# A hybrid encoder step on one core: TensorE's queue in the order in which the code emits it

## The chip, the core and the metric

The kernel runs on one core of one Trainium2 chip. The metric is the device time of one execution in microseconds (us); the time of a kernel is the median of its runs. The core has five engines with a queue each: TensorE (PE, with its weight loads as PEld), VectorE (DVE), ScalarE (ACT), GpSimd (POOL) and SyncE (SP), which here issues the transfers.

## What is computed

One layer of a streaming encoder, over a prompt of 2048 tokens and a sample of 32 tokens, all in float32. One projection yields the streams of two mixers: HGRN2, a gated recurrence of 4 heads evaluated in chunks of 64 tokens, and FoX, a causal attention of 8 heads with a forget gate. Then come an output projection, a second norm and a feed-forward block of width 4096.

```python
def mixer_inputs(x, norm1, w_in, ...):
    z = rms_norm(x, norm1) @ w_in
    qa, fa, ia, ga, qb, kb, vb, fb = jnp.split(z, SPLITS, axis=-1)
    ...
def mixer_output_and_ffn(x, o_a, ga, o_b, hgrn_out_norm, w_out, norm2, w_up, w_down):
    oa = rms_norm(o_a, hgrn_out_norm.reshape(A_HEADS, A_DV))
    oa = oa.reshape(B, T, A_WIDTH) * jax.nn.silu(ga)
    x = x + jnp.concatenate([oa, o_b], axis=-1) @ w_out
    h = rms_norm(x, norm2)
    return x + jnp.square(jax.nn.relu(h @ w_up)) @ w_down
```

The outputs are both sequences, the new keys, values and log forget values, and the recurrent states.

## The kernel before

**Tiles.** The prompt is cut into four quarters of 512 tokens; the third (`SQ`) carries the 32 sample tokens too and is worked in two pieces of 272. A dense product is made of three matmuls for each tile of 128 rows of weights (`mm3`): weights and activations are split into a rounded high part and the rest (`wh`, `wl`, `ahi`, `alo`), and high times high, high times low and low times high are added in one PSUM bank. `load_w` (L158) loads a weight strip, ACT rounds it to `wh` (L163), POOL subtracts to get `wl` (L165).

**PSUM.** Four pools share the eight banks: `ps_x` with three buffers (scores `st`, maxima `mx`, the recurrence's `xa`, `xu`, `xo`), `ps_o` with one (the attention's output `ot`), `ps_mm` with two for dense products, `ps_tr` with two for transposes (`ta`, `tk`, `tv`, `th`, `mt`, ...). Before the output projection, at L1327 and L1328, `ps_mm` and `ps_tr` are opened anew with three buffers and one.

**The flow.** All work is written as Python generators, and `Flow` (L41) decides in which order their instructions are emitted. It keeps a clock `flow.t` that only `mm` (L94) and `tp` (L102) advance, by an assumed time for each matmul or transpose. `dense` runs the main stream (strips of products) and, after each of its steps, everything whose due time has come: a generator that yields `lat` is taken up again `lat` us of that clock later. `until` runs only what is due until a condition holds. So the tails of a strip (transposes, norms, stores), the attention's steps and the norms are strewn between the matmuls of the strips.

**What sets the order on the engines.** What is emitted first has priority. But each engine's queue is written by the scheduler of the framework: it goes through the instructions with assumed durations, and when an engine is free it gives it the earliest emitted instruction that it takes to be ready, a later one where the earlier ones are not. The queue is fixed when the program is built; on the chip an engine goes through it in order, waiting on semaphores.

**Lines that the prediction follows.** `to_acts` (L190) transposes 128 tokens of the normed rows in two groups of four `ta`, with ACT's copy (L197) and DVE's subtraction (L198) behind each. `gate_tail` (L339) transposes the forget gate into `tl`, which ACT copies (L375). `att_max` (L828) takes row maxima, puts their negatives into `mpad` on DVE (L843, L844) and transposes them into `mt`. `out_tail` (L1083) and `y_tail` (L1165) bring a strip of the third quarter back to rows: four transposes, an add on DVE (L1087, L1175), then one more transpose for the sample tokens, in a new tile of the same pool:

```python
tr = ps_tr.tile([P, 4, P], F32, tag="tr", ...)
for i in range(4):
    tp(tr[:, i, :], ob[:, i * P:(i + 1) * P], ident)
dve.tensor_tensor(x2[:, :, cs], x2[:, :, cs], tr, op=ALU.add)
...
tr = ps_tr.tile([P, 4, P], F32, tag="tr", ...)
tp(tr[0:TS, 0, :], ob[:, 512:544], ident)
```

`ffn` (L1099) runs `up` (two strips of 128 of the 4096 columns) and `down` of the pair before in turn; after the last pair `down` follows at once.

Of the kernel before, what the change touches and what calls it, by code (L numbers as in the profile page):

```python
# [75 lines left out]
def hymba_step(  # L76
# [76 lines left out]
    def rstd(out, ss, n, cnt):  # L153

        pool.tensor_scalar(out, ss, 1.0 / cnt, EPS, op0=ALU.mult, op1=ALU.add)
        pool.tensor_tensor(out, out, phalf[0:out.shape[0], 0:n], op=ALU.pow)
# [22 lines left out]
    def nid():  # L179
        uid[0] += 1  # L180
        return uid[0]

    def new_acts(q):
        n = QN[q]
        u = nid()
        hi = acts.tile([P, KT, n], F32R, tag="ahi", name=f"ahi{u}")
        lo = acts.tile([P, KT, n], F32R, tag="alo", name=f"alo{u}")
        return hi, lo

    def to_acts(row, w, hi, lo, t0):  # L190

        for g in range(row.shape[1] // 512):
            tr = ps_tr.tile([P, 4, P], F32, tag="tr", name=f"ta{nid()}")
            for j in range(4):
                kt = 4 * g + j
                tp(tr[:, j, 0:w], row[0:w, kt * P:(kt + 1) * P], ident[0:w, 0:w])
            act.copy(hi[:, 4 * g:4 * g + 4, t0:t0 + w], tr[:, :, 0:w])  # L197
            dve.tensor_tensor(lo[:, 4 * g:4 * g + 4, t0:t0 + w], tr[:, :, 0:w],  # L198
                              hi.bitcast(F32)[:, 4 * g:4 * g + 4, t0:t0 + w], op=ALU.subtract)
            yield TLAT  # L200
# [6 lines left out]
    def load_gain(src):  # L207
        gb = const.tile([P, D], F32, tag="gbc", name=f"gbc{nid()}")
        sp.dma_start(gb, src.partition_broadcast(P))
        return gb  # L210
# [4 lines left out]
    def build(q, done, gb, getrow, src=None, first=False):  # L215

        while row_use:
            yield 0.5
        row_use.append(1)
        hi, lo = new_acts(q)  # L220

        if first:

            src = acts.tile([P, 4, D], F32, tag="ahi", name="stage")
            for i, (t0, w) in enumerate(QT[q]):
                sp.dma_start(src[:, i, :], getrow(q, t0, w))
                if i == 0:
                    gb = load_gain(norm1[0])
                    gains.append(gb)

        def prep(t0, w):
            if src is not None and t0 < 512:
                x = src[:, t0 // P, :]
                row = x if first else rows.tile([P, D], F32, tag="row", name=f"row{nid()}")
            else:
                row = rows.tile([P, D], F32, tag="row", name=f"row{nid()}")
                x = row
                sp.dma_start(row[0:w, :], getrow(q, t0, w))
            ss = small.tile([P, 2], F32, tag="ss", name=f"ss{nid()}")
            for g in range(2):  # L240
                junk = rows.tile([P, 512], BF16, tag="junk", name=f"junk{nid()}", bufs=1)
                act.activation(junk[0:w, :], x[0:w, 512 * g:512 * g + 512], AF.Square,
                               accum_out=ss[0:w, g:g + 1])
            r = small.tile([P, 1], F32, tag="rs", name=f"rs{nid()}")
            pool.tensor_tensor(r[0:w, :], ss[0:w, 0:1], ss[0:w, 1:2], op=ALU.add)
            rstd(r[0:w, :], r[0:w, :], 1, D)
            dve.scalar_tensor_tensor(out=row[0:w, :], in0=x[0:w, :], scalar=r[0:w, :],  # L247
                                     in1=gb[0:w, :], op0=ALU.mult, op1=ALU.mult)
            return row, w, t0

        lat = BLAT
        ts = QT[q]
        cur = prep(*ts[0])
        for i in range(len(ts)):
            nxt = prep(*ts[i + 1]) if i + 1 < len(ts) else None
            yield lat if i == 0 else lat - 3.0
            row, w, t0 = cur
            yield from to_acts(row, w, hi, lo, t0)
            cur = nxt
        done[q] = (hi, lo)  # L260
        row_use.clear()
# [938 lines left out]
    def heads(qs, hs, late=False):  # L1200
# [9 lines left out]
        for g in gates:  # L1210
            yield from g

    flow.spawn(build(0, A, None, xrow, None, True))
    flow.until(lambda: 0 in A)

# [142 lines left out]
    flow.until(lambda: 3 in H)  # L1358
    flow.dense(ffn(3, H, X, ffp))
    flow.until(lambda: not flow.q)  # L1360


# [31 lines left out]
```

## Time and profile before

| | |
|---|---|
| median of 3 runs | 2978.21 us (2977.03 to 2981.14) |
| the profiled execution | 2982.22 us, span 2980.5 us |
| TensorE matmuls busy | 2875.0 us, 96% |
| weight loads busy | 2435.9 us, 82% |
| VectorE, ScalarE, GpSimd busy | 62%, 46%, 37% |
| DMA queue of SP | 379.15 MB, 43.6% of 16 engines |

All rows are from one profiled execution. Its span runs from the first to the last recorded instruction, and times of places are counted from the span's start. In a timeline a row gives start, duration, engine, line, operation, out<-in, shapes and count, and in brackets the idle time of the engine before it with what ended it. Matmuls are pipelined: a row of TensorE lasts longer than the distance to the next one, so distances are taken from start to start. The granted clock is the share of TensorE's full 2.4 GHz that it was given; 0.50 is 1.2 GHz.

### The profile page before, as it was taken

The page shows a single profiled execution, that of the slowest core. Times are in us where ns is not written, and L with a number is a line of the kernel's source. Part 1 is how long each engine was busy: PE and PEld are TensorE (multiplying, and loading weights), DVE is VectorE, ACT ScalarE, POOL GpSimd, SP SyncE. Part 2 cuts the span into 40 slices and gives each one's busy share as a digit, 9 for nine tenths or more (in the row PEclk, how much of TensorE's full clock was granted, in tenths as well). Part 3 has the DMA queues.
Part 4 walks back from the last instruction along what each step waited for, and adds up shares of the span by engine and source line. Part 5 has one row for each costly group of instructions (what it writes and reads, how often), then busy time and mean ns, then how long its engine had stood idle before and what let it go on. Part 6 is the DMA issues. An engine that isn't in the chain of part 4 may idle for free.

```text
span 2980.5 us, 42522 instructions
## 1 busy us (share of the span) xinstructions
PE 2875.0 (96%) x15592; PEld 2435.9 (82%) x15592; DVE 1840.9 (62%) x3463; ACT 1368.4 (46%) x2391; POOL 1091.2 (37%) x600
## 2 busy tenths in 40 slices
PE   6899999899999999999999999999999999999999
PEld 5777777877788878888888888978899989988887
DVE  6447778776876777766666666566666554444333
ACT  4445566655555554544444444454444433222232
POOL 5452233434112334433333333333333344344443
PEclk9899999999999999999999999999999999999999
DMA  5663344656433564344335633443633333243333
GB/s 163 186 187 87 102 121 117 179 156 186 116 102 89 162 202 128 110 121 119 114 123 156 189 112 112 130 141 111 185 108 109 93 103 93 86 129 107 96 95 99
DMA packets 464143, 381.86 MB, mean 128 GB/s; under 512 B 34928, under 2 KB 363904, under 8 KB 463936
## 3 DMA queue, kind: packets, MB, share of 16 engines
q1 hardware_dynamic: 463936, 379.15, 43.6%
q8 instruction: 123, 2.02, 0.3%
q14 instruction: 84, 0.69, 0.1%
HBM read 316.67 MB, written 62.40 MB: 127 GB/s over the span
## 4 chain that ended last, share of the span: by engine, by line
PE 62%; DVE 1%; ACT 1%; issue 0%; POOL 0%; DMA 0%; SPq 0%; DVEq 0%; ACTq 0%; POOLq 0%
PE mm L100 54%; PE ot L100 3%; PE st L100 3%; PE mx L100 1%; PE ta L104 0%; PE rs L100 0%; ACT wh L163 0%; DMA row<-X 0%; DVE acc L1055 0%; PE tx L104 0%; POOL wl L165 0%; PE ty L104 0%; DVE os L916 0%; DVE ml L920 0%; DVE row L247 0%
## 5 line engine op out<-in xcount | busy, mean ns | idle before, releaser
L165 POOL TENSOR_TENSOR wl<-wr,wh 128x1024 fp32r<-128x1024 f32 x384 | 934.2, 2433 | 1685.7 <-ACT wh L163 1483.0
L100 PE MATMUL mm<-ahi,wh 128*128 128x512 f32 (+1 forms) x2528 | 899.0, 356 | 2.9 <-ACT t L512 1.6
L100 PE MATMUL mm<-ahi,wl 128*128 128x512 f32 (+1 forms) x2528 | 884.9, 350 | 1.5 <-POOL wl L165 1.5
L100 PE MATMUL mm<-alo,wh 128*128 128x512 f32 (+1 forms) x2528 | 885.8, 350 | 0.0
L163 ACT CAST wh<-wr 128x1024 fp32r<-128x1024 f32 x384 | 403.5, 1051 | 745.0 <-PE mm L100 645.3
L100 PEld LDWEIGHTS mm<-ahi,wh 128*128 128x128 f32 x2528 | 481.0, 190 | 63.2 <-DVE t L621 2.6
L100 PEld LDWEIGHTS mm<-ahi,wl 128*128 128x128 f32 x2528 | 479.7, 190 | 62.2 <-POOL wl L165 1.9
L100 PEld LDWEIGHTS mm<-alo,wh 128*128 128x128 f32 x2528 | 480.9, 190 | 57.3 <-issue 0.5
L1055 DVE TENSOR_TENSOR acc<-acc,mm 128x512 f32<-128x512 f32 x480 | 326.1, 683 | 155.7 <-PE mm L100 150.1
L879 ACT ACTIVATE st<-st 128x512 f32<-128x512 f32 (+1 forms) x320 | 169.3, 529 | 351.1 <-PE st L100 188.7
L883 DVE TENSOR_TENSOR pl<-st,ph 128x512 fp32r<-128x512 f32 (+1 forms) x320 | 198.2, 620 | 198.0 <-ACT ph L881 196.6
L100 PE MATMUL mm<-wh,uh 128*128 128x512 f32 x768 | 306.9, 400 | 2.8 <-DVE acc L1055 1.6
L100 PE MATMUL mm<-wh,ul 128*128 128x512 f32 x768 | 302.7, 395 | 0.0
L100 PE MATMUL mm<-wl,uh 128*128 128x512 f32 x768 | 302.5, 394 | 0.0
L1115 DVE TENSOR_TENSOR mm<-mm,r 128x512 f32<-128x512 f32 (+1 forms) x160 | 95.8, 599 | 291.0 <-ACT r L1114 289.1
L839 DVE TENSOR_REDUCE mc<-mx 128x1 f32<-128x512 f32 (+2 forms) x320 | 195.7, 617 | 36.9 <-PE mx L100 34.5
L100 PEld LDWEIGHTS mm<-wh,uh 128*128 128x128 f32 x768 | 144.6, 188 | 41.3 <-DVE acc L1055 7.5
L100 PEld LDWEIGHTS mm<-wh,ul 128*128 128x128 f32 x768 | 144.8, 189 | 35.2 <-DVE ul L1117 0.2
L887 DVE TENSOR_TENSOR acc<-acc,st 128x512 f32<-128x512 f32 (+2 forms) x288 | 173.3, 602 | 0.0
L881 ACT CAST ph<-st 128x512 fp32r<-128x512 f32 (+1 forms) x320 | 169.8, 532 | 7.2
L100 PEld LDWEIGHTS mm<-wl,uh 128*128 128x128 f32 x768 | 144.8, 189 | 30.8
L100 PE MATMUL mm<-uh,wh 128*128 128x272 f32 x512 | 149.6, 292 | 1.3 <-DVE acc L1148 1.3
(296 smaller groups left out, 4275.6 us busy)
## 6 DMA issues: line engine op xcount, KB each, us to landing
wr<-in_w_up_dram SPq DMA_DIRECT2D x128, 512.0 KB
wr<-in_w_down_dram SPq DMA_DIRECT2D x128, 512.0 KB
wr<-in_w_in_dram SPq DMA_DIRECT2D x96, 512.0 KB
kB<-KS SPq DMA_DIRECT2D x160, 128.0 KB
kA<-KS SPq DMA_DIRECT2D x80, 256.0 KB
V<-VS SPq DMA_DIRECT2D x80, 256.0 KB
wr<-in_w_out_dram SPq DMA_DIRECT2D x32, 512.0 KB
out_dram<-t SPq DMA_DIRECT2D x32, 256.0 KB
```

What stands on the lines that cost most here:

```text
L100: pe.matmul(out, lhsT, rhs, start=start, stop=stop)
L163: act.copy(hi, raw)
L165: pool.tensor_tensor(lo, raw, hi.bitcast(F32), op=ALU.subtract)
L839: dve.tensor_reduce(out=mc[:, j, kb:kb + 1], in_=mx[:, 0:n], axis=AX.X, op=ALU.max)
L879: act.activation(st[:, off:], st[:, off:], AF.Exp)
L881: act.copy(ph[:, off:], st[:, off:])
L883: dve.tensor_tensor(pl[:, off:], st[:, off:], ph.bitcast(F32)[:, off:], op=ALU.subtract)
L887: dve.tensor_tensor(acc[:, off:], acc[:, off:], st[:, off:], op=ALU.add)
L1055: dve.tensor_tensor(acc[:, t, c], acc[:, t, c], ps, op=ALU.add)
L1115: dve.tensor_tensor(z, z, r, op=ALU.mult)
```

## The change

A region is opened around the whole flow in which TensorE's instructions keep the order of their emission. The region names TensorE alone; the other engines, and the order across engines, stay with the scheduler. `mm` and `tp` emit the same calls in the same order as before.

```diff
@@ -1210,6 +1210,9 @@
+
+    mstack = ExitStack()
+    mstack.enter_context(tc.manual_schedule(engines={mybir.EngineType.PE}))
     flow.spawn(build(0, A, None, xrow, None, True))
     flow.until(lambda: 0 in A)
 
@@ -1358,6 +1361,7 @@
     flow.until(lambda: 3 in H)
     flow.dense(ffn(3, H, X, ffp))
     flow.until(lambda: not flow.q)
+    mstack.close()
```

## Rows read from the trace of the kernel before

**Rows 1.** The page's first part: busy us (share of the span) and instructions.

```profile
PE 2875.0 (96%) x15592; PEld 2435.9 (82%) x15592; DVE 1840.9 (62%) x3463; ACT 1368.4 (46%) x2391; POOL 1091.2 (37%) x600
```

**Rows 2.** The chain that ended last, share of the span by engine.

```profile
PE 62%; DVE 1%; ACT 1%; issue 0%; POOL 0%; DMA 0%; SPq 0%; DVEq 0%; ACTq 0%; POOLq 0%
```

**Rows 3.** Stretches: busy us and instructions by engine, granted clock, DMA share, GB/s.

```profile
0.00:75.00 75.00, 51.88 (x241) 39.15 (x241) 50.41 (x96) 37.03 (x76) 37.79 (x47) 1.00 0.59 162
75.00:225.00 150.00, 139.71 (x622) 112.76 (x623) 65.30 (x103) 68.62 (x114) 77.26 (x51) 0.94 0.68 185
225.00:1125.00 900.00, 839.85 (x4975) 703.31 (x4974) 671.05 (x1397) 519.90 (x1021) 273.36 (x169) 0.98 0.47 136
1125.00:1880.00 755.00, 753.53 (x3374) 616.86 (x3373) 493.45 (x827) 336.66 (x535) 282.67 (x137) 1.00 0.43 128
1880.00:2720.00 840.00, 834.04 (x5285) 758.06 (x5284) 465.94 (x899) 333.43 (x557) 311.97 (x152) 1.00 0.39 117
2720.00:2980.50 260.50, 255.98 (x1103) 205.78 (x1101) 94.73 (x142) 72.75 (x91) 108.11 (x45) 1.00 0.31 96
```

**Rows 4.** Timeline of TensorE: the first and the last displaced piece.

```profile
23.63 1.11 PE L104 MATMUL ta<-identr,stage 128*128 128x128 f32 x4 [0.57 <-DVE alo L198]
...
2966.66 0.50 PE L100 MATMUL mm<-wh,uh 128*128 128x512 f32 x1 [0.71 <-ACT uh L1116]
```

**Rows 5.** Timeline of TensorE from 362 to 368 us: a stop at `st`.

```profile
362.65 0.39 PE L100 MATMUL mm<-alo,wh 128*128 128x512 f32 x1
362.88 0.39 PE L100 MATMUL mm<-ahi,wl 128*128 128x512 f32 x1
366.67 0.44 PE L100 MATMUL st<-qC,kB 98*128 98x384 f32 x1 [3.40 <-DVE acc L885]
...
367.12 0.40 PE L100 MATMUL mm<-ahi,wh 128*128 128x512 f32 x1
367.36 0.40 PE L100 MATMUL mm<-alo,wh 128*128 128x512 f32 x1
```

**Rows 6.** Timeline, TensorE and DVE, of one of eight strips in `out_tail`.

```profile
1901.07 0.60 PE L104 MATMUL tx<-identr,ob 128*128 128x128 f32 x4
1901.43 0.38 PE L100 MATMUL mm<-ahi,wh 128*128 128x272 f32 x1
...
1901.71 0.69 DVE L1087 TENSOR_TENSOR acc<-acc,tx 128x512 f32<-128x512 f32 x1 [0.88 <-PE tx L104]
...
1902.50 0.28 PE L104 MATMUL tx<-identr,ob 128*32 128x128 f32 x1
```

**Rows 7.** Timeline, TensorE and DVE, of one of eight strips in `y_tail`.

```profile
2681.89 0.60 PE L104 MATMUL ty<-identr,acc 128*128 128x128 f32 x4
2682.25 0.48 PE L100 MATMUL mm<-wh,uh 128*128 128x512 f32 x1
...
2683.11 0.68 DVE L1175 TENSOR_TENSOR xy<-xy,ty 128x512 f32<-128x512 f32 x1
...
2684.19 0.28 PE L104 MATMUL ty<-identr,acc 128*32 128x128 f32 x1
```

**Rows 8.** Timeline, TensorE and DVE, around the transposes of `mpad`.

```profile
237.11 0.63 PE L100 MATMUL mm<-ahi,wh 128*128 128x512 f32 x1
...
241.87 0.15 DVE L844 TENSOR_TENSOR mpad<-nm,mpad 128x4 fp32r<-128x4 f32 x1
...
242.17 0.40 PE L104 MATMUL mt<-identr,mpad 128*2 128x128 f32 x4 [0.37 <-DVE hcc L638]
```

**Rows 9.** Timeline, TensorE and ACT, around one group of `ta`.

```profile
522.72 0.39 PE L100 MATMUL mm<-ahi,wh 128*128 128x272 f32 x1
...
525.51 0.57 ACT L375 COPY t<-tl 8x512 f32<-8x512 f32 x1
...
530.16 0.66 PE L104 MATMUL tk<-identr,t 128*128 128x128 f32 x4 [1.15 <-DVE alo L198]
```

**Rows 10.** Stretches as in rows 3: two idle ones, each with what follows it.

```profile
230.60:233.70 3.10, 0.00 (x0) 0.00 (x0) 3.07 (x10) 2.25 (x5) 0.00 (x0) 1.00 0.14 43
235.16:238.57 3.41, 3.41 (x10) 2.67 (x9) 3.29 (x7) 0.67 (x2) 0.00 (x0) 0.50 0.65 153
...
540.90:543.20 2.30, 0.00 (x0) 0.00 (x0) 2.30 (x2) 1.54 (x5) 1.84 (x2) 1.00 0.00 0
543.30:546.70 3.40, 3.40 (x25) 3.19 (x25) 3.37 (x7) 2.65 (x5) 0.74 (x2) 1.00 0.92 202
```

## The prediction

> **What bounds the kernel now.** I read the page's busy line first, then the shares of the chain of waits by engine, then the busy time of each engine by stage, and last the timeline of TensorE at single places. The busy line says that TensorE's matmuls fill 96% of the span and nothing else comes near [rows 1]; the chain that ended last is TensorE by 62%, with 1% each for VectorE and ScalarE [rows 2]. By stage there are two kernels in one. Up to 1125 us (input projections, recurrent heads, first half of the attention) TensorE idles 23.1 us in the start, 10.3 us up to 225 us and 60.2 us up to 1125 us. From 1125 us on it idles 1.5, 6.0 and 4.5 us in 1855 us [rows 3]. So in the first part a stop may stand in for another stop; in the second part every stop of TensorE is added to the time.
>
> **What the change touches.** It adds no instruction, no byte and no tile. It takes one freedom away. In the kernel before, every engine's queue is filled by the scheduler, which takes the earliest emitted instruction that it holds to be ready; where that one is not ready in its own reckoning, TensorE is given a later one. With the change TensorE issues in the order in which `mm` and `tp` are called. DVE, ACT, POOL and SP keep the scheduler's order, and no DMA is moved by the edit itself.
>
> How far apart are the two orders? The flow's clock `flow.t` is plain arithmetic, so the order of the calls can be followed in the code and laid beside the order of the records. Nine matmuls in ten stand where they were emitted. The others lie in 106 places, the first with a transpose `ta` at 23.63 us, the last with the product `mm<-wh,uh` at 2966.66 us [rows 4], and each has one form: a piece X (a few transposes or one product) was not ready when its turn came, and a number of later matmuls, 2 to some 120, went ahead of it. What each place costs in the new order is the time from the start of the first matmul that went ahead to the end of the DVE or ACT instruction on which X hung, less the idle time that TensorE spends there already. The work that went ahead is not lost; it comes afterwards, and all behind it with it.
>
> **That a waiting instruction holds TensorE** can be seen before the change. At 362.88 us a strip's matmul is issued and at 366.67 us the attention's `st`, after 3.40 us of idle that DVE ended; the strip goes on only behind it, at 367.12 us, though it lacked nothing [rows 5]. Whatever stands at the head waits, and the rest with it. So the price of a place is an idle gap.
>
> **Places with one answer: `tx` and `ty`.** `out_tail` writes four transposes into a tile of `ps_tr`, lets DVE add them (L1087), and takes a tile of the same pool for the fifth transpose, with no `yield` between. From L1328 on (`ps_tr2`) that pool has one buffer, so the fifth waits for the add. Before, six matmuls and an `st` went in between: the first of them starts at 1901.43 us and the add ends at 1901.71 + 0.69 = 1902.40 us, which makes 0.97 us [rows 6]. There are eight strips, each so: 8 x 0.97 = 7.8 us. `y_tail` has the same form with L1175. Four of its eight are as long as this; in the other four DVE has an accumulation in hand, and the add ends at 2683.11 + 0.68 = 2683.79 us, 1.54 us after the first matmul that went ahead at 2682.25 us [rows 7]: 4 x 0.97 + 4 x 1.54 = 10.0 us. Together 17.8 us, in a stage with 6.0 us of idle in 840 us [rows 3]. What would cover it is a matmul in between, and that is what the change takes away.
>
> **The other places.** In the second part 29 more: transposes of the second norm and of the attention and products that wait for an accumulator, 0 to 1.6 us each, and the end of each of the four `ffn`s, where `down` follows `up` at once and waits for the squares, 0.8 to 2.1 us. They sum to 16.5 us. The second part costs 17.8 + 16.5 = 34.3 us.
>
> In the first part 61 places sum to 50.8 us. The largest are of two kinds. The `mt` transposes hang on DVE's `mpad`: the first strip matmul to go ahead starts at 237.11 us, DVE ends `mpad` at 241.87 + 0.15 = 242.02 us, so TensorE would stop for 4.9 us where it stops for 0.4 now [rows 8]: 4.5 us. The `ta` transposes hang on a tile of `ps_tr` that ACT still reads: from 522.72 us to 525.51 + 0.57 = 526.08 us, 3.4 us [rows 9]. Fifty-nine more lie between -0.4 and 4.0 us.
>
> Here stops replace stops. X ends no later in the new order than in the old one, and what hangs on X neither; only the matmuls that went ahead, and what follows them, come later. So a wait soon after on something that hangs on X shrinks by as much: behind the place at 526 us TensorE waits 1.15 us at 530.16 us for the evacuation of that same `ta` [rows 9], and when it arrives 3.4 us later that wait is gone. The trace cannot show how much of the 50.8 us goes that way. Bounds: nothing of it (50.8 us stay) and three quarters of it (13 us stay, since the idle from 75 to 1125 us, 70.5 us, is in part the waits that are to be replaced). I take half, 25 us, because 35 of the 61 places follow another within 10 us, so that the shift of the one is time that the next no longer has to wait.
>
> **The clock.** Idle costs a second time in the first part. The granted clock is 0.94 in 75 to 225 us and 0.98 in 225 to 1125 us, and 1.00 from there on [rows 3]. After an idle stretch of 3.1 us the clock stands at its lower level, 1.2 GHz, from 235.16 to 238.57 us; after one of 2.3 us it stays at 2.4 GHz [rows 10]. From 0.94 and 0.98, the granted clock falls short by 0.06 x 150 + 0.02 x 900 = 27 us of full-speed time for 70.5 us of idle: 0.38 us for each us. For 25 us more idle that is 9 us; the ends are 0 (no gap long enough is added) and 0.38 x 50.8 = 19 us. In the second part the gaps are short and the row shows no loss at them.
>
> **Sum.** 25 + 34 + 9 = 68 us. The profiled execution took 2982.2 us (span 2980.5 us), 4 us over the median of 2978.2 us; the stops are the same in both, so I add them to the median: 2978 + 68 = 3046 us. Lower end: 13 + 27 (a fifth of the second part caught up by the engines that TensorE waits for) + 0 = 40, 3018 us; upper end: 51 + 34 + 19 + 6 (from release to start at some 60 places with a true stop, 0.10 us each, as between the end of the add at 1902.40 us and `tx` at 1902.50 us [rows 6]) = 110, 3088 us.
>
> **The rivals.**
> *Only the second part pays.* In the first part DVE is busy for 671 of 900 us [rows 3] and TensorE's pauses there are waits for a late DVE; if DVE sets the pace of that part, more waiting at one place is less at the next, and 34 us or less remain: 3000 to 3015 us. For it: both large kinds above are DVE or ACT running late. Against: DVE is a quarter idle. Chance 0.14.
> *The clock falls too.* If most of the stops of over 2 us each bring a stretch at the lower level and these slow down what follows, the first part keeps its 51 us and loses 30 or more: 3090 to 3130 us. For it: gaps of that length precede the low stretch of rows 10. Against: the second gap there, which does nothing. Chance 0.07.
> *The stops vanish in TensorE's slack.* If the 96% hide room, a stopped queue runs faster afterwards and nothing changes: 2978 us, within 6 us. Weight loads fill 82% of the span [rows 1]. Against: after the stop of 3.40 us the strip's matmuls come 0.24 us apart (367.12, 367.36 us), before it 0.23 us (362.65, 362.88 us); they do not catch up [rows 5]. With it goes the case that the edit moves nothing in the queue. The Trainium skill, Perfetto Trace Analysis, section Identifying the Most-Contended Engine, calls matmul busy time a poor measure of nearness to the roof and has headroom judged by the utilisation in FLOPs and the weight loads' busy share; by that rule the 82% leave 18% of room. The row decides against it here: the room is not used after a stop. Chance 0.05.
> *Faster: the chains start earlier.* X is issued the moment it is ready, ahead of the matmuls that were let through, so DVE and ACT get their next piece sooner and the pauses of the first part dissolve. It decides when it removes more than the 34 us that the second part adds, that is when over half of the 70.5 us of idle between 75 and 1125 us goes and none is added. With all of it gone: 2978 - 70.5 + 34 = 2942 us. Against: at nearly all of the 106 places the producer ends after X's turn, so X gains only the length of one matmul or so. Chance 0.03.
>
> **How the numbers follow.** The forecast, 3018 to 3088 us, has 0.71; its point is 3046 us. The range takes in the larger part of the first rival: 3004 to 3090 us, which leaves out about 0.17. A change of 0.2% (6 us) is what a measurement of this kernel can tell from none. Slower 0.92, within 0.2% 0.05, faster 0.03.
>
> **What would show it.** Right: `tx` and `ty` each stand directly behind their first four, with a wait of about 1 to 1.5 us put down to DVE L1087 and L1175; TensorE's idle after 1125 us rises from 12 to about 45 us; `mt` follows the matmul at its emitted place with a wait of several us on `mpad`; the idle up to 1125 us rises by less than 51 us. Wrong: idle after 1125 us that stays under 25 us, or idle up to 1125 us that falls. If TensorE's idle rises as forecast and the time does not, the step that fails is that a stop is added to the time.

## The result and the profile after

| | before | after |
|---|---|---|
| median of 4 runs, us | 2979.68 (2977.03 to 2981.74) | 3057.18 (3049.63 to 3059.69) |
| profiled execution, span, us | 2980.5 | 3047.9 |
| matmuls busy, us | 2875.0 | 2883.2 |
| TensorE idle (span less busy), us | 105.5 | 164.7 |
| mean granted clock | 0.990 | 0.986 |

The kernel after takes 1.0256 times as long [1.0236, 1.0277], 77 us more. The profiled execution of after is the shortest of its four. It is 67.4 us longer than the profiled one of before, and this divides into 164.7 - 105.5 = 59.2 us of idle and 2883.2 - 2875.0 = 8.2 us of the same 15592 matmuls lasting longer. The other three runs of after have spans of 3054 to 3058 us at clocks of 0.983 to 0.985; 0.002 of 2883 us of matmuls is 6 us, which would be most of the 6 to 10 us that part them from the profiled one.

The first part of the page and the chain's shares by engine in the kernel after, to be laid beside [rows 1] and [rows 2]:

```profile
PE 2883.2 (95%) x15592; PEld 2441.7 (80%) x15592; DVE 1846.7 (61%) x3463; ACT 1371.4 (45%) x2391; POOL 1085.6 (36%) x600
...
PE 60%; DVE 3%; ACT 1%; issue 1%; DMA 0%; POOL 0%; SPq 0%; DVEq 0%; ACTq 0%; POOLq 0%
```

The instruction counts are the same. On the chain, TensorE gives 2% of the span to VectorE: places where matmuls used to stand and where the chain now passes through a DVE instruction.

The stretches of [rows 3] in the kernel after, each cut where the same matmul of the order of emission starts (columns as there):

```profile
0.00:74.30 74.30, 51.92 (x241) 40.12 (x241) 50.35 (x96) 37.13 (x76) 36.56 (x47) 0.95 0.59 163
74.30:221.20 146.90, 135.47 (x622) 109.07 (x623) 65.08 (x103) 68.25 (x114) 77.26 (x51) 0.98 0.69 189
221.20:1152.50 931.30, 843.73 (x4974) 709.95 (x4973) 671.05 (x1395) 522.46 (x1021) 271.05 (x169) 0.97 0.46 131
1152.50:1915.30 762.80, 755.37 (x3375) 616.38 (x3374) 495.24 (x829) 336.87 (x536) 282.26 (x137) 1.00 0.43 127
1915.30:2786.40 871.10, 840.56 (x5285) 760.52 (x5284) 470.09 (x899) 334.02 (x557) 310.39 (x152) 1.00 0.38 112
2786.40:3047.90 261.50, 256.16 (x1103) 205.66 (x1101) 94.88 (x142) 72.65 (x91) 108.11 (x45) 1.00 0.32 96
```

TensorE's idle is the length less the first busy figure. Against [rows 3] it goes from 23.1, 10.3, 60.2, 1.5, 6.0, 4.5 us to 22.4, 11.4, 87.6, 7.4, 30.5, 5.3 us. The first three stretches gain 27.8 us of idle and 27.5 us of length, the last three 31.2 us of idle and 39.9 us of length.

What TensorE waits for in the kernel after (line waited for, us in total, times, longest):

```profile
PE ta L104 <- DVE alo L198: 17.8, 12, 4.1
PE st L100 <- DVE acc L887: 13.8, 6, 4.7
...
PE ty L104 <- DVE xy L1175: 8.5, 8, 1.4
...
PE tx L104 <- DVE acc L1087: 6.3, 8, 0.8
PE mt L104 <- DVE mpad L844: 6.2, 2, 4.8
```

`ty` and `tx` are not in that list before, where `ta` has 9.3 us and `st` behind L887 5.5 us. A place in `out_tail` in the kernel after (timeline, TensorE and DVE), and the row of one of the longer stops in `y_tail`:

```profile
1937.35 0.60 PE L104 MATMUL tx<-identr,ob 128*128 128x128 f32 x4
...
1937.98 0.69 DVE L1087 TENSOR_TENSOR acc<-acc,tx 128x512 f32<-128x512 f32 x1 [0.88 <-PE tx L104]
...
1938.72 0.28 PE L104 MATMUL tx<-identr,ob 128*32 128x128 f32 x1 [0.78 <-DVE acc L1087]
1938.76 0.37 PE L100 MATMUL mm<-ahi,wh 128*128 128x272 f32 x1
...
2746.22 0.28 PE L104 MATMUL ty<-identr,acc 128*32 128x128 f32 x1 [1.36 <-DVE xy L1175]
```

The product that stood right behind the four transposes in [rows 6] now stands behind the fifth, after 0.78 us of nothing.

Laid side by side by line and tile, about one in ten of the 15592 matmuls of the two traces stands at another place. The other engines' queues are not untouched: about a tenth of the instructions of DVE, of ACT and of SP stand elsewhere too, since the scheduler plans them around the new order.

### The profile page after: what moved, and what is told of

Read it like the earlier page. It is cut to its first block, busy times and chain, and to the rows that moved or that the text cites. A ratio compares the mean times of both kernels' runs of the same rounds, so it can differ in the third digit from the quotient of the medians.

```text
span 3047.9 us, 42525 instructions
## 1 busy us (share of the span) xinstructions
PE 2883.2 (95%) x15592; PEld 2441.7 (80%) x15592; DVE 1846.7 (61%) x3463; ACT 1371.4 (45%) x2391; POOL 1085.6 (36%) x600
## 4 chain that ended last, share of the span: by engine, by line
PE 60%; DVE 3%; ACT 1%; issue 1%; DMA 0%; POOL 0%; SPq 0%; DVEq 0%; ACTq 0%; POOLq 0%
PE mm L100 52%; PE st L100 3%; PE ot L100 3%; PE mx L100 1%; PE ta L104 0%; DVE acc L1055 0%; DVE pl L883 0%; DVE acc L887 0%; DVE row L247 0%; ACT wh L163 0%; DVE mm L1115 0%; PE ty L104 0%; PE rs L100 0%; DVE alo L198 0%; DMA row<-X 0%
## 5 line engine op out<-in xcount | busy, mean ns | idle before, releaser
L165 POOL TENSOR_TENSOR wl<-wr,wh 128x1024 fp32r<-128x1024 f32 x384 | 931.3, 2425 | 1745.0 <-ACT wh L163 1541.1
L887 DVE TENSOR_TENSOR acc<-acc,st 128x512 f32<-128x512 f32 (+2 forms) x288 | 173.6, 603 | 0.0
```

Of the source, the lines that this page charges most:

```text
L165: pool.tensor_tensor(lo, raw, hi.bitcast(F32), op=ALU.subtract)
L887: dve.tensor_tensor(acc[:, off:], acc[:, off:], st[:, off:], op=ALU.add)
```

## The experiments

**Which part pays: the region over one part alone.** In the first of these two kernels the region is opened only ahead of the closing of the pools at L1325, near 1100 us; in the second it is closed there.

```diff
-    mstack = ExitStack()
-    mstack.enter_context(tc.manual_schedule(engines={mybir.EngineType.PE}))
     flow.spawn(build(0, A, None, xrow, None, True))
...
+    mstack = ExitStack()
+    mstack.enter_context(tc.manual_schedule(engines={mybir.EngineType.PE}))
     tmp_stack.close()
```

> TensorE keeps the order of emission only from the point where the temporary tiles are given back (about 1090 us) to the end; before that point the scheduler orders it as in the kernel before. Theory (each stop of TensorE is added, place by place): plus 38 us by the sum of the places from 1090 us on (34.3 + 4.0), plus 41 us by the shift measured between the two profiles from there on: 3018 to 3023 us. Rival 1 (the loss comes from the other engines' queues, of which the first half holds most of the displaced instructions): plus 20 us or less. Rival 2 (the clock makes most of the loss): plus 10 us or less, since the granted clock is 1.00 in this part of both profiles.

Measured: 3023.6 us, ratio 1.0151 [1.0136, 1.0166], 43.7 us over before. Both rivals fall, and the cost is at the upper end of what was expected. In the two traces TensorE's order is that of before ahead of the place where the region opens and that of after behind it.

```diff
     flow.until(lambda: all(g == HA for g in hg_done) and sample_done)
+    mstack.close()
     tmp_stack.close()
...
     flow.until(lambda: not flow.q)
-    mstack.close()
```

> The order of emission only up to about 1090 us; after it the scheduler orders TensorE as in the kernel before. Theory: plus 26 us (the shift measured between the two profiles at 1088 us) to plus 36 us (what the medians, 77 us apart, leave when the second part takes 41): 3006 to 3016 us. The parts add up: the gains over before of this run and of the second-part run sum to the 77 us within 10. Rival 1 and 2: plus 50 us or more.

Measured: 3012.15 us, ratio 1.0110 [1.0095, 1.0125], 32.3 us over before. The two make 76 us, the whole change 77 us, each known to some 5 us: each part pays for itself, and nothing shows that one gives the other anything back. The two halves of the kernel with the region in the second part alone, and then those of before (columns as in the stretches above):

```profile
0.00:1100.00 1100.00, 1002.62 (x5728) 833.79 (x5729) 767.23 (x1557) 618.22 (x1199) 378.70 (x264) 0.98 0.51 142
1100.00:3021.50 1921.50, 1878.33 (x9866) 1604.12 (x9864) 1077.69 (x1906) 750.65 (x1193) 709.33 (x337) 1.00 0.40 118
```

```profile
0.00:1100.00 1100.00, 1007.63 (x5735) 835.97 (x5736) 771.11 (x1566) 618.97 (x1200) 378.84 (x263) 0.97 0.50 140
1100.00:2980.50 1880.50, 1867.36 (x9858) 1599.95 (x9857) 1069.77 (x1898) 749.43 (x1191) 712.31 (x337) 1.00 0.40 121
```

In the second part idle rises from 13.1 to 43.2 us, by 30.1 us, and busy by 11.0 us. The idle is near the 34 us of the prediction; the 11 us of busy time, of which the eight more matmuls in the stretch make some 2 us, stood in no term for this part.

**Are the stops of `tx` and `ty` worth their length?** The flow is told to let other work out between the add and the fifth transpose, first in the kernel after, then in the one before.

```diff
         dve.tensor_tensor(x2[:, :, cs], x2[:, :, cs], tr, op=ALU.add)
         sp.dma_start(X2[0:512, cs].rearrange("(t p) c -> p t c", p=P), x2[:, :, cs])
+        yield 1.3
...
             sp.dma_start(yp[q * 512:(q + 1) * 512, cs].rearrange("(t p) c -> p t c", p=P), xt[:, 0:4, :])
+            yield 1.9
```

> The changed kernel with one yield each (1.3 and 1.9 us of the flow's clock) put between the first four transposes and the fifth in the tails of the third quarter, so that matmuls are emitted in between. Theory: the 16 stops measured as 0.97 to 1.5 us each go, minus 17 to 19 us against the changed kernel: 3038 to 3040 us. Rival 1: within 5 us of the changed kernel, because those stops only move.

Measured: 3051.24 us, ratio 1.0240 [1.0224, 1.0255], 6 us less than after where some 18 were expected, and the intervals of the two ratios overlap, so that it may be less. TensorE no longer waits ahead of any `tx` or `ty`; something else came.

> The same two yields in the kernel before, where the scheduler orders TensorE. Theory: nothing, within 5 us of before, because the scheduler already puts matmuls in between. Rival 1 (the yields are a gain of their own, whoever orders TensorE): minus 15 us or more.

Measured: 2981.59 us, ratio 1.0008 [0.9998, 1.0018]. Where the scheduler fills the gaps itself, the hint is worth nothing.

To tell apart whether the stops are cheap or the hint dear, the next kernel leaves the order of the calls as it is and takes away what the fifth transpose waits for: its tile comes from `ps_x`, which has three buffers. In the trace TensorE's order is that of after, matmul by matmul.

```diff
-        tr = ps_tr.tile([P, 4, P], F32, tag="tr", name=f"tx{nid()}")
+        tr = ps_x.tile([P, 4, P], F32, tag="x", name=f"tx{nid()}")
...
-            tr = ps_tr.tile([P, 4, P], F32, tag="tr", name=f"ty{nid()}")
+            tr = ps_x.tile([P, 4, P], F32, tag="x", name=f"ty{nid()}")
```

> The changed kernel, but the fifth transpose of each tail takes a buffer of ps_x in place of the one buffer of ps_tr. Nothing is moved in the order of emission. Theory (a stop is worth its length, and the run with the two yields gave back only 6 us because the yields made the second norm's input late and brought new stops): the stops go without moving anything, minus 15 to 20 us against the changed kernel, 3037 to 3042 us. Rival (a stop taken away comes back at the next wait, since another engine sets the pace): minus 8 us or less, as with the yields.

Measured: 3038.42 us, ratio 1.0194 [1.0180, 1.0208], 18.8 us less than after. In its timeline the fifth transpose follows the four so closely that one row holds all five, and DVE's add comes after it:

```profile
1940.35 0.71 PE L104 MATMUL tx<-identr,ob 128*128 128x128 f32 x5
1940.98 0.69 DVE L1087 TENSOR_TENSOR acc<-acc,tx 128x512 f32<-128x512 f32 x1 [0.88 <-PE tx L104]
```

So the stops, 14.8 us of idle in the kernel after, cost at least about what they last, and the hint is dear. The 18.8 us are known to some 7 us. The other side of the same question makes them longer, by a second pass of DVE over the tile ahead of the add in both tails:

```diff
+        dve.tensor_scalar(tr, tr, 1.0, None, op0=ALU.mult)
         dve.tensor_tensor(x2[:, :, cs], x2[:, :, cs], tr, op=ALU.add)
```

> The changed kernel with one more DVE pass over the same PSUM bank (times 1.0, in place) ahead of the add in each of the 16 tails, so that each of the 16 stops grows by one DVE instruction of about 0.6 us start to start. Theory: plus 9 to 11 us against the changed kernel, 3066 to 3068 us. Rival (stops are taken up elsewhere): within 3 us of the changed kernel.

Measured: 3072.89 us, ratio 1.0317 [1.0301, 1.0333], 15.7 us over after. The direction is the expected one, the size was taken too low. The same place as above in this kernel:

```profile
1944.14 0.60 PE L104 MATMUL tx<-identr,ob 128*128 128x128 f32 x4
1944.77 0.70 DVE L1087 TENSOR_SCALAR tx<-tx 128x512 f32<-128x512 f32 x1 [0.88 <-PE tx L104]
1945.51 0.69 DVE L1088 TENSOR_TENSOR acc<-acc,tx 128x512 f32<-128x512 f32 x1
...
1946.34 0.27 PE L104 MATMUL tx<-identr,ob 128*32 128x128 f32 x1 [1.60 <-DVE acc L1088]
```

The stop grows from 0.78 to 1.60 us. Over all sixteen, TensorE's idle ahead of `tx` and `ty` goes from 14.8 to 30.3 us, 15.5 us more, and the time by 15.7 us. That the two agree to 0.2 us is luck, since by the ratios the 15.7 us are 18 us, known to some 8; the size is that of the stops.

> The same extra DVE pass in the kernel before. Theory: nothing, within 3 us of before, since matmuls lie between the add and the fifth transpose there. If it costs 9 us or more here too, the price is DVE's and not the order's.

Measured: 2981.33 us, ratio 1.0005 [0.9993, 1.0016]. The same 16 passes of DVE cost nothing that can be measured where the scheduler orders TensorE: behind the four transposes at 1904.83 us of this trace it lets out ten matmuls ahead of the fifth, where it let out seven in [rows 6]. This pair is the change in small: DVE's added work is the same, and what decides is whether TensorE has something else at the head of its queue.

**Where the hint in `out_tail` loses its gain.** The hint is given in `y_tail` alone (the second of the two lines above).

> The changed kernel with the yield in the last tail (y_tail) alone; nothing waits for its result but the store. Theory: its eight stops (9.8 us by the shift between the two profiles over that stretch) go and nothing new comes: minus 9 to 10 us against the changed kernel, 3047 to 3048 us. So the loss in the run with both yields comes from the other tail. Rival: minus 3 us, half of what both yields gave.

Measured: 3048.72 us, ratio 1.0227 [1.0213, 1.0241], 8.5 us less than after, a little less than expected. It is 2.5 us shorter than with both hints; the intervals overlap, so the times alone do not show that the hint in `out_tail` costs anything, only that its eight stops bring no gain. The profiled executions show more. The stretch of `out_tail` and the one behind it: the kernel after, the one with both hints, the one with the hint in `y_tail` alone:

```profile
1920.00:1998.00 78.00, 71.73 (x501) 66.12 (x500) 33.15 (x58) 32.01 (x61) 23.78 (x15) 1.00 0.41 120
1998.00:2050.00 52.00, 45.29 (x213) 36.20 (x212) 37.33 (x60) 26.02 (x50) 17.97 (x16) 0.93 0.47 135
```

```profile
1927.00:2005.00 78.00, 76.17 (x524) 70.46 (x522) 40.05 (x70) 37.57 (x72) 29.24 (x22) 1.00 0.46 131
2005.00:2060.00 55.00, 44.83 (x183) 35.24 (x184) 35.31 (x49) 20.25 (x35) 12.95 (x8) 0.84 0.40 118
```

```profile
1920.00:1998.00 78.00, 72.50 (x498) 66.70 (x497) 35.30 (x58) 31.36 (x55) 21.38 (x9) 1.00 0.41 119
1998.00:2050.00 52.00, 44.74 (x217) 36.48 (x216) 36.16 (x59) 28.41 (x56) 20.36 (x21) 0.95 0.48 141
```

With both hints the first stretch idles 1.8 instead of 6.3 us. The second idles 10.2 instead of 6.7 us, and its clock is 0.84 instead of 0.93: 0.16 x 55 - 0.07 x 52 = 5.2 us of full-speed time more. By this estimate 4.5 us are won and 3.5 + 5.2 = 8.7 us lost. Two stops of the second stretch, in the kernel with both hints and then in the kernel after:

```profile
2023.89 0.58 PE L104 MATMUL mt<-identr,mpad 128*2 128x128 f32 x4 [4.07 <-DVE alo L198]
...
2051.59 1.11 PE L104 MATMUL ta<-identr,row 128*128 128x128 f32 x4 [5.00 <-DVE alo L198]
```

```profile
2018.86 0.40 PE L104 MATMUL mt<-identr,mpad 128*2 128x128 f32 x4 [0.72 <-DVE alo L198]
...
2038.13 1.11 PE L104 MATMUL ta<-identr,row 128*128 128x128 f32 x4 [4.11 <-DVE alo L198]
```

With the hint in `y_tail` alone these two stops are 0.73 and 3.86 us, as in the kernel after. The strips that `out_tail` brings back are the input of the second norm, and each hint puts a strip's end later; so `ta` and `mt`, which hang on that norm, can reach the head of the queue before their data. At the stop at `mt`, which grew most, two things can be read. In the kernel after nine matmuls stand between the last `ta` (2015.46 us) and `mt`; with both hints `ta` is emitted later (2019.22 us) and `mt` stands right behind it. And DVE takes longer to reach the subtraction. Rows of POOL and DVE in the kernel with both hints and then in the kernel after:

```profile
2020.34 2.35 POOL L165 TENSOR_TENSOR wl<-wr,wh 128x1024 fp32r<-128x1024 f32 x1 [5.64 <-ACT wh L163]
2020.81 2.42 DVE L905 TENSOR_TENSOR acl<-acc,ach 128x512 fp32r<-128x512 f32 x1
2023.16 0.68 DVE L198 TENSOR_TENSOR alo<-ta,ahi 128x512 fp32r<-128x512 f32 x1
```

```profile
2018.03 0.68 DVE L198 TENSOR_TENSOR alo<-ta,ahi 128x512 fp32r<-128x512 f32 x1
...
2019.22 1.85 DVE L905 TENSOR_TENSOR acl<-acc,ach 128x512 fp32r<-128x512 f32 x1
```

The subtraction that `mt` waits for stands ahead of L905 in the kernel after. With both hints it stands behind it, and L905, whose median is 0.69 us, lasts 2.42 us beside POOL. So the order of TensorE and that of DVE both have a part in this stop, and no run parts them. What was won at one place was lost at the next.

**Do truer assumed times help the order of emission?** In `to_acts` the flow assumes 1.2 us for one group of `ta`. It is raised, in the kernel before and in the one with the other pool:

```diff
-    BLAT, TLAT, MLAT = 7.5, 1.2, 4.0
+    BLAT, TLAT, MLAT = 7.5, 2.0, 4.0
```

> The kernel before, with the flow's assumed time for one group of transposes in to_acts raised from 1.2 to 2.0 us, so that more matmuls are emitted between one group of ta and the next. In the kernel before TensorE waits 9.3 us in all for the subtraction of L198 ahead of ta. If those waits come from the emission being too close, up to 9.3 us go: 2972 to 2977 us. If the scheduler fills these gaps as far as there is work, whatever the emission says, nothing moves: 2976 to 2984 us.

Measured: 2980.47 us, ratio 0.9996 [0.9987, 1.0005]. TensorE waits 8.8 us instead of 9.3 us ahead of these `ta`. The first expectation falls.

> The kernel after, with the fifth transposes on the other pool (as in e5) and the flow's assumed time for one group of transposes in to_acts raised from 1.2 to 2.0 us. In e5 TensorE waits 15.9 us at 12 places ahead of ta for L198. Theory: in the order of emission the assumed times are what keeps a waiting piece away from the head of the queue, so the truer figure takes away about half of that: 3028 to 3034 us, against 3038 us for e5. Rival: every later piece of the norm and what hangs on it comes later as well, as with the yield in out_tail, and the stops move on instead of going: 3036 to 3046 us.

Measured: 3030.28 us, ratio 1.0166 [1.0152, 1.0180], by the ratios some 8 us less than with the other pool alone (their intervals just touch); the profiled executions are only 2.7 us apart (spans of 3032.3 and 3035.0 us). What TensorE waits for with the other pool alone, and then with the raised figure too:

```profile
PE ta L104 <- DVE alo L198: 15.9, 12, 3.6
...
PE mm L100 <- DVE acc L1055: 10.6, 4, 7.3
```

```profile
PE mm L100 <- DVE acc L1055: 15.3, 8, 7.8
...
PE ta L104 <- DVE alo L198: 9.7, 5, 4.3
```

6.2 us of waits go from `ta`, and 4.7 us more stand at `mm`; part of the gain was moved on. So in the order of emission the assumed time seems to matter, by an amount that these runs do not settle; with the scheduler the same raise changes nothing that can be measured. None of these kernels comes below the time before: the best one that keeps the order of emission throughout is still 1.7% longer.

## Why the prediction was right, and which of its steps were not

**That the stop at the head is added to the time** held. The longer and the removed stops of `tx` and `ty` decide it for these sixteen places, with the same DVE work in the kernel before as the counter-proof (15.7 us against 0.7 us). For the other places it rests on the idle that came, with the region; of these only the `ta` were shortened by an edit, with part of the gain moved on. The rival of the slack falls with it: weight loads fill 80% of the span after the change, and 15.5 us more of stops still made 15.7 us more of time. The Trainium skill, Perfetto Trace Analysis, section Identifying the Most-Contended Engine, has TensorE's headroom judged by the FLOP rate and the weight loads' busy share. It does not say that such room makes up for a stop, and here it did not.

**`tx` and `ty`.** 17.8 us were forecast and 18.8 us went with the other pool. The stops themselves are shorter than forecast, 6.3 and 8.5 us instead of 7.8 and 10.0. In [rows 6] the next matmul starts 0.36 us after the row of the four transposes does; in the kernel after the fifth starts 1938.72 - 1937.35 = 1.37 us after it. So 1.01 us are lost at this place, of which 0.78 us show as idle: a row of TensorE lasts longer than the distance to the next one, and at a stop its last 0.23 us are not covered and count as busy. As a price the count from start to start was the better one.

**The second part.** 34 us of idle were forecast for 1125 us to the end, and the idle there went from 12 to 43.2 us where 45 was named as the sign. Without the 14.8 us at `tx` and `ty` the idle rose by 16.4 us, where 16.5 were forecast for the 29 other places. Its whole cost is larger, 39.9 us in the profiled execution and 43.7 us with the region there alone.

**The first part.** Half of 50.8 us, 25 us, was taken, and 27.8 us of idle came; with the region there alone the cost was 32.3 us. The rival by which only the second part pays falls with that. That the half was nearly right does not show each place right. At the place of [rows 9] 3.4 us were forecast:

```profile
530.85 0.90 PE L104 MATMUL ta<-identr,row 128*128 128x128 f32 x4 [2.52 <-ACT t L375]
...
538.35 0.60 PE L104 MATMUL tk<-identr,t 128*128 128x128 f32 x4
```

2.52 us came, and ahead of `tk` no wait is left of the 1.15 us, as forecast: a stop that took the place of another. At the place of [rows 8] 4.9 us were forecast, and 1.36 us came (TensorE and DVE):

```profile
233.50 0.63 PE L100 MATMUL mm<-ahi,wl 128*128 128x512 f32 x1
...
234.69 0.15 DVE L635 TENSOR_TENSOR hcc<-he 128x4 f32<-128x4 f32 x1
...
235.19 0.16 DVE L844 TENSOR_TENSOR mpad<-nm,mpad 128x4 fp32r<-128x4 f32 x1
...
235.49 0.40 PE L104 MATMUL mt<-identr,mpad 128*2 128x128 f32 x4 [1.36 <-DVE mpad L844]
```

The step that failed here is "X ends no later in the new order than in the old one", taken as if it ended at the same time: from the first matmul to the end of `mpad` it is 1.85 us (233.50 to 235.19 + 0.16) instead of 4.9. 2.2 of the 3.1 us are one short instruction of DVE ahead of it, which lasts 0.15 instead of 2.36 us (the last section has the rows of both). Other `mt` do stop for long, one for 4.8 us. The half held as a sum; the two places looked at came out below their price, so that the sum held is in part luck.

**The clock.** 9 us were forecast, all in the first part, since "in the second part the gaps are short and the row shows no loss at them". Worked out as in the prediction, the granted clock of the first part now falls short by 0.05 x 74.3 + 0.02 x 146.9 + 0.03 x 931.3 = 35 us instead of 27: 8 us more, near the forecast. Behind the stop of 2.52 us above, for one, the clock is at 1.2 GHz:

```profile
531.10:534.50 3.40, 3.40 (x18) 3.40 (x17) 2.92 (x5) 2.61 (x5) 0.06 (x1) 0.50 0.92 295
```

The step that failed is that this is added to the time of the first part. The matmuls there sum to 1031.1 us after and 1031.4 before, and its length grew by no more than its idle; what made up for the slower stretches is open. The 8.2 us by which the matmuls did become longer are all in the second part, at 1852.1 us after and 1843.6 before, where as whole stretches the clock stands at 1.00 in both and the prediction had no term. Of these 8.5 us, 16 x 0.23 = 3.7 us are the uncovered ends at `tx` and `ty` of the paragraph above, an estimate from one place. Some 2 us are clock: the stop of 4.11 us at `ta` lies in the 52 us from 1998 us on, at 0.93, which loses 0.07 x 52 = 3.6 us; the same work before stood at 0.97:

```profile
1957.00:2010.00 53.00, 50.32 (x237) 39.92 (x236) 39.27 (x66) 26.99 (x49) 20.59 (x16) 0.97 0.47 140
```

which loses 1.6 us. The other stops of the second part should leave ends uncovered too; these were not counted. So it is partly luck that 68 us were forecast and the profiled executions are 67.4 us apart: 9 us that the first part did not show stand against 8.5 us that nobody forecast for the second.

In the first part the clock differs from run to run: from 74 to 222 us the profiled execution of before had 0.94, the two kernels of before with an edit in the tails alone, whose TensorE order is the same up to 1894 us, had 0.98 and 0.95, and the kernel after 0.98. 0.04 x 148 = 6 us, as much as the term itself, and why it differs is open. So what the clock costs in the first part is not settled by one profile of each. The 10 us by which the difference of the medians exceeds that of the profiled executions may belong here, since the longer runs have the lower clocks; it is not shown.

**The other engines.** "No DMA is moved by the edit itself" was too simple: about a tenth of DVE's and of SP's instructions changed places. What this costs or gives over the whole kernel was not tried by itself; the stop at `mt` in the kernel with both hints shows a longer stop with another order of DVE ahead of it.

## What to carry to other kernels

Where one engine is nearly always busy, its queue should hold something else between a producer and its consumer; if the scheduler's reordering provides that, fixing the order costs each of those gaps once, and in a stretch with next to no idle the sum over the displaced pieces, worked out from start to producer's end, was a usable forecast (34.3 us forecast, 31.2 us of idle). In a stretch that already has stops, a part of the new ones replaces old ones: here about 28 to 32 us of 51 were paid. Here a gap was better closed by taking away what the waiting instruction needs (a buffer of another pool) than by sending other work ahead by hand, after which longer stops stood at the next place.

## What the runs showed of the hardware

A DVE instruction on a few elements can last as long as one of POOL that runs beside it. In the kernel before and then in the kernel after (DVE and POOL):

```profile
239.33 2.39 POOL L165 TENSOR_TENSOR wl<-wr,wh 128x1024 fp32r<-128x1024 f32 x1 [11.47 <-ACT wh L163]
...
239.37 2.36 DVE L635 TENSOR_TENSOR hcc<-he 128x4 f32<-128x4 f32 x1
```

```profile
237.66 2.67 POOL L165 TENSOR_TENSOR wl<-wr,wh 128x1024 fp32r<-128x1024 f32 x1 [13.55 <-ACT wh L163]
...
238.01 2.60 DVE L645 TENSOR_TENSOR qx<-t,hcc 128x256 f32<-128x256 f32 x1
```

The four columns of L635 took 0.15 us in the kernel after, with POOL at rest, and 2.36 us in the kernel before, ending with POOL's subtraction. In the kernel after another instruction, L645, is the one caught in this way. So a small shift in time can take 2 us from a chain or add them, and a producer's end read in one trace does not hold for another order. In the trace of before, 52 instructions of DVE last over 1 us more than the median of their line and shape, and every one of them overlaps an instruction of POOL, which is busy for 37% of the span. Not every instruction beside POOL is slowed: of the 68 of L198 there, 24 start while POOL works, and none lasts over 0.69 us. That the two engines share something is argued from these rows; no run took POOL's instruction away.
